# The output gate of a gated recurrence: multiplied by features in the output projection instead of by tokens in the recurrence

## The chip, the cores and the metric

The kernel runs on one core of one Trainium2 chip. The metric is the device time of one execution in microseconds; the time of a kernel is the median of its runs. A core has TensorE (PE in the profile, matrix products and transposes), VectorE (DVE), ScalarE (ACT), GpSimd (POOL) and SyncE (SP). SP does nothing here but issue loads, POOL issues the stores. Every engine executes its own instructions in the order in which they stand, and waits on semaphores for the others.

## What is computed

One layer of a language model on 2048 tokens of 1024 features. A combined input projection feeds two groups of heads, whose outputs are concatenated, multiplied by an output matrix and added to the residual with a layer norm behind it. The change lies in the first group, a gated linear recurrence with four heads of 128 features, of which this is the core:

```
h = jnp.einsum('btd,de->bte', h_res, w_in[layer])
hq, hf, hi, hg, aq, ak, av, ag = jnp.split(h, IN_SPLITS, axis=-1)
...
o_h = hgrn2_chunk(rs(q_h), rs(k_in), rs(hi.astype(f32)), rs(log_f))
o_h = o_h * lax.rsqrt(jnp.mean(o_h * o_h, axis=-1, keepdims=True) + RMS_EPS)
o_h = o_h * hg_norm_w[layer].astype(f32).reshape(HG_HEADS, HG_HEAD_DIM)
o_h = o_h.reshape(B, T, HG_WIDTH).astype(dt) * jax.nn.silu(hg)
...
mix = jnp.concatenate([o_h, o_a], axis=-1)
out = jnp.einsum('bte,ed->btd', mix, w_out[layer])
z = DN_ALPHA * h_res.astype(f32) + out.astype(f32)
```

`hi` are the values of the recurrence and `hg` its gate. The gate multiplies each head's normalised output, feature by feature.

## The kernel before

**Input projection.** The projection's columns are 26 feature tiles of 128 features, taken in 13 pairs. The tokens are two superblocks of 1024 (s = 0, 1), each two blocks of 512 tokens. One pair on one superblock is a 2x2 block product, computed with seven products of the Strassen-Winograd kind instead of eight: `px`, `py` and `pz` are its PSUM tiles, s1, s2, s5 and c10 the SBUF copies and sums that are formed from them, and `Pair.joined` (L364) adds a PSUM tile to such a copy. Every fp32 operand is split into a high and a low part of type fp32r, so a product is 12 matmuls of 128x512 (L342 to L344). A superblock takes 91 slots, one product each. The operand tiles of the weights (`w`) are made from loads of `in_wt_dram` in the first superblock and kept in DRAM (`kw`); the second superblock loads these 512 KB tiles.

**finish (L306).** A feature tile comes out with features on the partitions and 512 tokens along the row. `finish` stores it to DRAM as `proj[w][b]`, w being the feature tile and b the block of 512 tokens. Tiles 10 to 25 belong to the recurrence: of every eight (for a pair of heads j) two are forget gates (10, 11), two queries (12, 13), two values (14, 15) and two output gates (16, 17); 18 to 25 are the same for the second pair. They are stored as they are. Tiles 3, 4, 8 and 9, gates of the other group, go through SiLU by features first (`th`, L314 and L315: t · (1 + tanh(t/2)), the factor one half being left for later).

**Units.** Beside the products run 16 units of work, attached to slots by the table `units_at` (L790): 8 of `attend(j, b)`, which is the other group, and 8 of `recur(j, b)`. `recur` loads forget gates and queries (r10, r12, ...), forms decays by scans on DVE (`e`, L561 and L562), a reciprocal (L571) and the products `kq`. Its values and gates come by `fetch_vg` (four loads of 128 KB for two chunks of 128 tokens) and `vg`: for each chunk two heads' values and two heads' gates are transposed to have tokens on the partitions (eight transposes for two chunks), the values are copied out of PSUM by ACT, the gates get tanh on ACT and a product on DVE. `chunk` makes the outputs `ho` (L659), normalises them per token to `om`, multiplies by the gate (L675) and stores to `hg_spill`.

**Output stage.** There are 16 token tiles n of 128 tokens. `out_prepare(n)` is called one tile ahead: it loads the recurrence's output `mh` and the other group's output `ms` for these tokens, transposes the first in PE to features by tokens (`mp`, in a PSUM ring with one buffer, which the recurrence's `kp` shares), and splits both into high and low parts `m_0h`, `m_0l`, `m_1h`, `m_1l` (L724, L725). `out_tile(n)` does 48 matmuls of 128x512 into two PSUM tiles `po`, then residual and layer norm (`xr`). The output weights `wo` take the places of the input's operand tiles. Two of the recurrence's units still run while the first output tiles are computed.

**Order.** The program is written slot by slot, and a scheduler then sets the order of each engine's instructions by a list schedule with priorities; the joins and the copies of the products are marked high priority. A small change of the program can thus reorder work at a distance.

Of the kernel before, what the change touches and what calls it, by code (L numbers as in the profile page):

```python
# [13 lines left out]
AF = mybir.ActivationFunctionType  # L14
# [3 lines left out]
P = 128  # L18
# [26 lines left out]
def tile_hybrid_layer(  # L45
# [119 lines left out]
    def t_tile(name, dt=F32):  # L165
        return ring.tile([P, 512], dt, tag="t", name=name, bufs=9)
# [139 lines left out]
    def finish(pair, row, col, s, t):  # L306
        w, b = pair[col], 2 * s + row
        if w >= 10:
            nc.gpsimd.dma_start(proj[w][b], t)  # L309
            return  # L310
        j, kind = w // 5, w % 5
        if kind >= 3:
# [223 lines left out]
    def recur(j, b):  # L536
# [46 lines left out]
        def fetch_vg(pr):  # L583
            got["vg"] = []
            for i in range(2):
                t = t_tile(f"vg{j}_{b}_{pr}_{i}").rearrange("p (h t) -> p h t", t=2 * P)
                for h in range(2):
                    nc.sync.dma_start(t[:, h], proj[14 + 8 * j + 2 * i + h][b][:, pr * 2 * P : (pr + 1) * 2 * P])
                got["vg"].append(t)

        def vg(pr):
            raw = got["vg"]
            v4 = t_tile(f"hv{j}_{b}_{pr}").rearrange("p (s t) -> p s t", t=P)
            g4 = t_tile(f"hg{j}_{b}_{pr}").rearrange("p (s t) -> p s t", t=P)
            for i in range(2):
                c = 2 * pr + i
                ps = mm_ps(f"vg{j}_{b}_{c}").rearrange("p (s t) -> p s t", t=P)
                for s in range(4):
                    nc.tensor.transpose(ps[:, s, :], raw[s // 2][:, s % 2, i * P : (i + 1) * P], ident)
                nc.scalar.activation(v4[:, 2 * i : 2 * i + 2], ps[:, 0:2], AF.Copy)  # L600
                g = g4[:, 2 * i : 2 * i + 2]
                nc.scalar.activation(g, ps[:, 2:4], AF.Tanh, scale=0.5)
                nc.vector.scalar_tensor_tensor(g, g, 1.0, ps[:, 2:4], op0=ALU.add, op1=ALU.mult)
            got["v", pr] = v4, g4
# [31 lines left out]
        def chunk(c):  # L636
            pr, i = c // 2, c % 2
            at, kt = got["kt"]
            v4, g4 = got["v", pr]
# [35 lines left out]
            nc.vector.tensor_mul(om, om, g4)  # L675
# [7 lines left out]
            [lambda: factors(1), lambda: fetch_vg(0)],  # L683
            [],
            [lambda: vg(0), lambda: inner(0)],
            [lambda: chunk(0), lambda: fetch_vg(1)],
            [lambda: chunk(1)],
            [lambda: vg(1), lambda: inner(1)],
# [23 lines left out]
    def out_prepare(n):  # L712
# [7 lines left out]
        mp = mp.rearrange("p e t -> p (e t)")  # L720
        out_ = []
        for k, src in enumerate((mp, sw)):
# [210 lines left out]
```

## Time and profile before

| | before |
|---|---|
| time, median of 3 runs | 959.62 us (954.17 to 961.7) |
| the profiled execution's own time | 956.75 us |
| its span in the profile | 955.0 us |
| mean granted TensorE clock | 0.971 of full |

A profile is one execution. Its engines' rows say when an instruction ran and for how long; a matmul's row includes its latency, so neighbours overlap. "Granted clock" is the TensorE clock in parts of full speed.

### The profile page before, as it was taken

The numbers are of one execution on the slowest core, as the hardware profiler recorded it, in microseconds if no ns is written. First come the engines' busy times: TensorE is split into PE (matmuls) and PEld (weight loads), VectorE is DVE, ScalarE is ACT, GpSimd is POOL, SyncE is SP. The second block draws the span as 40 slices with busy tenths as digits, with TensorE's granted clock in tenths as the row PEclk, the third lists the DMA queues.
The fourth block names the chain that finished last, engine by engine and source line by source line (L and its number), as shares of the span: only waits on it lengthen the run. The fifth ranks groups of instructions, "written<-read, shape, count | busy, mean of one in ns | idle before, by whom it ended". The sixth has DMA issues, their size and how long they took to land.

```text
span 955.0 us, 14480 instructions
## 1 busy us (share of the span) xinstructions
PE 890.1 (93%) x4542; PEld 708.8 (74%) x4542; DVE 634.7 (66%) x1272; ACT 460.8 (48%) x1236; POOL 270.4 (28%) x444
## 2 busy tenths in 40 slices
PE   8478999999999999869999999989998999999995
PEld 6356777776778887658786768867787888888884
DVE  5977577575686589658565565445786889766554
ACT  5434455354553565428663535435576544544311
POOL 2224333333332222243422222222221232222211
PEclk9879999999999999979999999999999999999998
DMA  9289978675376675875958595475688534543222
GB/s 311 88 275 328 305 274 266 221 231 208 146 271 226 238 273 161 319 255 204 305 197 227 186 300 177 135 231 175 233 297 287 166 118 170 162 152 126 81 95 82
DMA packets 94493, 203.04 MB, mean 213 GB/s; under 512 B 13776, under 2 KB 31312, under 8 KB 94416
## 3 DMA queue, kind: packets, MB, share of 16 engines
q1 hardware_dynamic: 70448, 123.44, 41.9%
q0 software_dynamic: 23680, 78.15, 22.0%
q8 instruction: 36, 0.59, 0.3%
q10 hardware_dynamic: 288, 0.52, 0.1%
q14 instruction: 41, 0.34, 0.1%
HBM read 120.92 MB, written 78.64 MB: 209 GB/s over the span
## 4 chain that ended last, share of the span: by engine, by line
PE 70%; DMA 13%; DVE 9%; issue 3%; SPq 3%; ACT 2%; POOL 0%; DVEq 0%; POOLq 0%; ACTq 0%
PE px L342 7%; PE px L343 7%; PE px L344 7%; PE po L752 6%; PE po L753 6%; PE po L754 6%; PE pz L342 4%; PE pz L343 4%; PE pz L344 4%; DMA w<-in_wt_dram 3%; PE op L508 3%; DMA w<-kw 2%; PE sp L458 1%; PE sp L459 1%; PE hkv L647 1%
## 5 line engine op out<-in xcount | busy, mean ns | idle before, releaser
L309 POOL DMA_DIRECT2D proj<-s x48 | 26.6, 555 | 114.1 <-DVE s L364 86.3
L571 DVE RECIPROCAL f<-e 128x512 f32<-128x512 f32 x16 | 53.5, 3342 | 0.1
L359 ACT ACTIVATE s<-px 128x512 f32<-128x512 f32 x52 | 31.1, 598 | 45.3 <-PE px L344 37.7
L481 POOL TENSOR_TENSOR wt<-wt,st 128x512 f32<-128x512 f32 x32 | 34.0, 1062 | 62.1 <-DVE st L480 59.3
L472 ACT ACTIVATE wt<-sp,st 128x129 f32<-128x129 f32 x128 | 45.3, 369 | 4.1 <-DVE st L468 3.7
L766 ACT ACTIVATE xr<-xr,rs 128x512 f32<-128x512 f32 x32 | 24.3, 808 | 46.3 <-DVE rs L763 46.2
L185 DVE TENSOR_TENSOR w<-w,w 128x512 fp32r<-128x512 f32 x43 | 32.8, 769 | 16.3 <-ACT w L184 16.1
L755 DVE SCALAR_TENSOR_TENSOR xr<-xr,po 128x512 f32<-128x512 f32 x32 | 21.8, 682 | 29.8 <-PE po L754 27.7
L467 ACT ACTIVATE sp<-sink 128x2 f32<-128x2 f32 x64 | 11.1, 176 | 62.7 <-DVE st L464 59.1
L458 PE MATMUL sp<-kh,qa 128*128 128x256 f32 (+1 forms) x128 | 33.9, 295 | 7.2 <-DMA qa<-hl 5.6
L303 POOL DMA_DIRECT2D kw<-w x52 | 28.5, 547 | 39.7 <-DVE w L185 36.8
L342 PE MATMUL px<-x_s20h,w 128*128 128x512 f32 x26 | 12.2, 469 | 28.5 <-ACT w L184 23.8
L184 ACT ACTIVATE w<-w 128x512 fp32r<-128x512 f32 x43 | 26.9, 629 | 22.9 <-PE px L344 9.9
L463 DVE COPY_PREDICATED sp<-past,sp 128x256 f32<-128x256 int32 x60 | 24.6, 423 | 19.8 <-PE sp L459 19.6
L518 POOL DMA_DIRECT2D sw_spill<-mix x32 | 17.9, 561 | 63.6 <-DVE mix L517 51.8
L631 ACT ACTIVATE u<-s,e 128x128 f32<-128x128 f32 x60 | 21.4, 396 | 27.3 <-DVE s L656 22.9
L769 POOL DMA_DIRECT2D out_dram<-xr x30 | 17.6, 586 | 57.2 <-DVE xr L768 53.4
L493 ACT ACTIVATE pall<-pt 128x512 f32<-128x512 f32 x32 | 19.1, 596 | 30.1 <-PE pt L490 29.4
L459 PE MATMUL sp<-kl,qa 128*128 128x256 f32 (+1 forms) x128 | 33.4, 292 | 0.0
L517 DVE TENSOR_TENSOR mix<-op,gate 128x128 f32<-128x128 f32 x64 | 15.4, 282 | 26.9 <-PE op L508 26.1
L458 PEld LDWEIGHTS sp<-kh,qa 128*128 128x128 f32 x128 | 24.4, 193 | 11.8 <-DMA qa<-hl 7.9
L359 ACT ACTIVATE c<-px 128x512 f32<-128x512 f32 x26 | 15.6, 600 | 29.3 <-PE px L344 24.7
(506 smaller groups left out, 3169.1 us busy)
## 6 DMA issues: line engine op xcount, KB each, us to landing
kw<-w POOLq DMA_DIRECT2D x52, 512.0 KB, 4.8
w<-kw SPq DMA_DIRECT2D x52, 512.0 KB, 4.5
proj<-s POOLq DMA_DIRECT2D x60, 256.0 KB, 3.8
w<-in_wt_dram SPq DMA_DIRECT2D x47, 256.0 KB, 4.7
r<-proj SPq DMA_DIRECT2D x32, 256.0 KB, 4.2
vg<-proj SPq DMA_DIRECT2D x64, 128.0 KB, 4.1
xr<-in_xn_dram SPq DMA_DIRECT2D x32, 256.0 KB, 3.0
out_dram<-xr POOLq DMA_DIRECT2D x30, 256.0 KB, 2.5
```

Source lines behind the costliest of these rows:

```text
L342: nc.tensor.matmul(ps, lhsT=ah, rhs=bh, start=start, stop=False, skip_group_check=not first)
L343: nc.tensor.matmul(ps, lhsT=ah, rhs=bl, start=False, stop=False, skip_group_check=not first)
L344: nc.tensor.matmul(ps, lhsT=al, rhs=bh, start=False, stop=q == 3, skip_group_check=not first)
L359: nc.scalar.activation(t, ps, AF.Copy)
L458: nc.tensor.matmul(sp[:, h, lo:], lhsT=lhs, rhs=kh[:, kc], start=True, stop=False)
L459: nc.tensor.matmul(sp[:, h, lo:], lhsT=lhs, rhs=kl[:, kc], start=False, stop=True)
L472: nc.scalar.activation(wt_[:, s, :], sps[s // 2][:, s % 2, P - 1 :], AF.Exp, bias=st[:, 1, s : s + 1], scale=0.125, accum_out=st[:, 2, s : ...
L481: nc.gpsimd.tensor_mul(wt_[:, :, 1:], wt_[:, :, 1:], st[:, 0, :].unsqueeze(2).to_broadcast([P, 4, P]))
L571: nc.vector.reciprocal(re, e[:, :, 1:129])
L752: nc.tensor.matmul(ps, lhsT=h[:, q], rhs=wh, start=e == 0, stop=False)
L753: nc.tensor.matmul(ps, lhsT=h[:, q], rhs=wl, start=False, stop=False)
L754: nc.tensor.matmul(ps, lhsT=l[:, q], rhs=wh, start=False, stop=e == 7)
```

## The change

The gate tiles 16, 17, 24 and 25 go through SiLU in `finish`, by features, like the other group's gates. The recurrence then loads and transposes only values (`fetch_v`, `values`), eight fewer transposes in each of the eight units, and stores its outputs without the gate. In `out_prepare` the gate tile `gm` of the token tile is loaded (four loads of 64 KB, L712 of the changed kernel), and DVE multiplies the transposed outputs in PSUM with it; the high and low parts are split from the product in SBUF.

```diff
     def finish(pair, row, col, s, t):
         w, b = pair[col], 2 * s + row
-        if w >= 10:
+        if w >= 10 and (w - 10) % 8 < 6:
             nc.gpsimd.dma_start(proj[w][b], t)
             return
         j, kind = w // 5, w % 5
-        if kind >= 3:
+        if w >= 10 or kind >= 3:
             th = t_tile(f"th{w}_{b}")
...
-        def fetch_vg(pr):
-            got["vg"] = []
-            for i in range(2):
-                t = t_tile(f"vg{j}_{b}_{pr}_{i}").rearrange("p (h t) -> p h t", t=2 * P)
-                for h in range(2):
-                    nc.sync.dma_start(t[:, h], proj[14 + 8 * j + 2 * i + h][b][:, pr * 2 * P : (pr + 1) * 2 * P])
-                got["vg"].append(t)
-
-        def vg(pr):
-            raw = got["vg"]
+        def fetch_v(pr):
+            got["raw"] = t_tile(f"v{j}_{b}_{pr}").rearrange("p (h t) -> p h t", t=2 * P)
+            for h in range(2):
+                nc.sync.dma_start(got["raw"][:, h], proj[14 + 8 * j + h][b][:, pr * 2 * P : (pr + 1) * 2 * P])
+
+        def values(pr):
+            raw = got["raw"]
             v4 = t_tile(f"hv{j}_{b}_{pr}").rearrange("p (s t) -> p s t", t=P)
-            g4 = t_tile(f"hg{j}_{b}_{pr}").rearrange("p (s t) -> p s t", t=P)
-            for i in range(2):
-                c = 2 * pr + i
-                ps = mm_ps(f"vg{j}_{b}_{c}").rearrange("p (s t) -> p s t", t=P)
-                for s in range(4):
-                    nc.tensor.transpose(ps[:, s, :], raw[s // 2][:, s % 2, i * P : (i + 1) * P], ident)
-                nc.scalar.activation(v4[:, 2 * i : 2 * i + 2], ps[:, 0:2], AF.Copy)
-                g = g4[:, 2 * i : 2 * i + 2]
-                nc.scalar.activation(g, ps[:, 2:4], AF.Tanh, scale=0.5)
-                nc.vector.scalar_tensor_tensor(g, g, 1.0, ps[:, 2:4], op0=ALU.add, op1=ALU.mult)
-            got["v", pr] = v4, g4
+            ps = mm_ps(f"vp{j}_{b}_{pr}").rearrange("p (s t) -> p s t", t=P)
+            for s in range(4):
+                nc.tensor.transpose(ps[:, s, :], raw[:, s % 2, (s // 2) * P : (s // 2 + 1) * P], ident)
+            nc.scalar.activation(v4, ps, AF.Copy)
+            got["v", pr] = v4
...
-            nc.vector.tensor_mul(om, om, g4)
             nc.gpsimd.dma_start(
...
         for e in range(4):
             nc.tensor.transpose(mp[:, e, :], m[:, e * P : (e + 1) * P], ident)
-        mp = mp.rearrange("p e t -> p (e t)")
+        gated = t_tile(f"gm{n}").rearrange("p (e t) -> p e t", t=P)
+        for e in range(4):
+            nc.sync.dma_start(gated[:, e], proj[16 + 8 * (e // 2) + e % 2][n // 4][:, (n % 4) * P : (n % 4 + 1) * P])
+        nc.vector.tensor_mul(gated, mp, gated)
         out_ = []
-        for k, src in enumerate((mp, sw)):
+        for k, src in enumerate((gated.rearrange("p e t -> p (e t)"), sw)):
             h, l = m_split(src, f"m{n}_{k}")
```

The scheduler's order moves with it. In the rows below a name ends in a running number, and what an instruction waits for stands in brackets. The first place is the start of the second token superblock, SP's loads; `w1_0_7` is an operand tile of superblock 1, pair 0, product 7, and `r10_1` the forget gates of block 1. Before:

```order
L287 DMA w1_0_7_3858<-kw0_7_226 128x1024 [waits DMASW5_49,DMASW7_49,DMASW2_49,PE_49]
L259 DMA w1_8_1a_4357<-in_wt_dram 128x512 [waits DMAHW5_49,DVE_49]
L287 DMA w1_0_4_3920<-kw0_4_223 128x1024 [waits DMASW3_49,DMAHW6_49,DMASW2_49,PE_49]
L542 DMA r10_1_3881<-proj10_1_160 128x512 [waits DMAHW7_49,Pool_49]
L542 DMA r12_1_3883<-proj12_1_168 128x512 [waits DMAHW0_49]
L287 DMA w1_1_6_3964<-kw1_6_229 128x1024 [waits DMAHW1_49,PE_49]
```

After, on the same engine:

```order
L287 DMA w1_0_7_3852<-kw0_7_226 128x1024 [waits DMASW7_49,DMAHW0_49,DMASW4_49,PE_49]
L287 DMA w1_0_4_3914<-kw0_4_223 128x1024 [waits DMASW2_49,DMAHW1_49,DMASW0_49,PE_49]
L287 DMA w1_1_6_3958<-kw1_6_229 128x1024 [waits DMAHW4_49,DMAHW2_49,PE_49]
L259 DMA w1_8_1a_4333<-in_wt_dram 128x512 [waits DMAHW3_49,DVE_49]
L542 DMA r10_1_3875<-proj10_1_160 128x512
L542 DMA r12_1_3877<-proj12_1_168 128x512 [waits DMAHW5_49,Pool_49]
```

The loads r10_1 and r12_1 have moved behind w1_1_6, and w1_8_1a behind w1_1_6 as well. In the same place on DVE, before; `e0_1` are the scans, `s5_1_0` the joins of superblock 1, pair 0:

```order
L561 SCALAR_TENSOR_TENSOR e0_1_3879<-f0_1_3886 128x64
L364 TENSOR_TENSOR s5_1_0_3979<-px1_0_3681,s5_1_0_3979 128x512
L562 SCALAR_TENSOR_TENSOR e0_1_3879<-f0_1_3886 128x64
...
L185 TENSOR_TENSOR l6_2_3915<-s1_1_6_3800,h6_2_3914 128x512
L571 RECIPROCAL f0_1_3886<-e0_1_3879 128x512
L577 SCALAR_TENSOR_TENSOR r12_1_3883<-tq0_1_3939,r12_1_3883 128x512
L364 TENSOR_TENSOR s2_1_0_3934<-pz1_0_3966,s2_1_0_3934 128x512
```

And after:

```order
L562 SCALAR_TENSOR_TENSOR e0_1_3873<-f0_1_3880 128x64
L185 TENSOR_TENSOR l6_2_3909<-s1_1_6_3794,h6_2_3908 128x512
L571 RECIPROCAL f0_1_3880<-e0_1_3873 128x512
L577 SCALAR_TENSOR_TENSOR r12_1_3877<-tq0_1_3933,r12_1_3877 128x512
L364 TENSOR_TENSOR s5_1_0_3973<-px1_0_3675,s5_1_0_3973 128x512
L185 TENSOR_TENSOR w1_1_3_4048<-w1_2_1_3956,w1_1_3_4048 128x512
L364 TENSOR_TENSOR s2_1_0_3928<-pz1_0_3960,s2_1_0_3928 128x512
```

The join s5_1_0 has moved from between the first scans to behind the reciprocal and r12's product. The second place is the head of the output stage, SP's loads before:

```order
L716 DMA mh0_7446<-hg_spill0_0_95 128x256 [waits DMAHW2_49,DVE_49]
...
L716 DMA mh1_7465<-hg_spill0_1_96 128x256
L588 DMA vg0_3_1_0_7546<-proj14_3_178 128x256 [waits DMAHW5_49,Pool_49]
L716 DMA ms1_7466<-sw_spill1_0_65 128x256 [waits DMAHW6_49,DVE_49]
L716 DMA ms1_7466<-sw_spill1_1_66 128x256 [waits DMAHW7_49]
L588 DMA vg0_3_1_0_7546<-proj15_3_182 128x256 [waits DMAHW0_49]
```

After, on SP:

```order
L706 DMA mh0_7330<-hg_spill0_0_95 128x256 [waits DMAHW4_49,DMAHW1_49,DVE_49]
...
L706 DMA mh1_7355<-hg_spill0_1_96 128x256
L735 DMA xr0_0_7384<-in_xn_dram 128x512 [waits DMASW7_49,DMASW4_49,DMAHW7_49,DMASW2_49,DMASW0_49]
L706 DMA ms1_7356<-sw_spill1_0_65 128x256 [waits DMAHW1_49,DMAHW2_49,DMAHW0_49,PE_49]
L706 DMA ms1_7356<-sw_spill1_1_66 128x256
L712 DMA gm0_7341<-proj16_0_183 128x128
L712 DMA gm0_7341<-proj17_0_187 128x128 [waits DMAHW3_49]
L712 DMA gm0_7341<-proj24_0_215 128x128 [waits DMAHW4_49]
L712 DMA gm0_7341<-proj25_0_219 128x128 [waits DMAHW5_49]
```

The gate loads gm0 stand behind the loads ms1, whose wait is now for PE (its transposes mp0) where it was for DVE. PE at the same place, before:

```order
L719 MATMUL mp0_7452<-ident_294,mh0_7446 128x128
L659 MATMUL ho0_3_0_7528<-hv0_3_0_7395,at0_348 128x128 [waits DVE_49,Activation_49]
...
L659 MATMUL ho0_3_0_7528<-hv0_3_0_7395,at0_348 128x128
L752 MATMUL po0_0_7493<-wo_a110h_7125,m0_0h_7457 128x512 [waits Activation_49]
L753 MATMUL po0_0_7493<-wo_a110l_7126,m0_0h_7457 128x512
```

And after:

```order
L709 MATMUL mp0_7336<-ident_294,mh0_7330 128x128
L650 MATMUL ho0_3_0_7424<-hv0_3_0_7287,at0_348 128x128 [waits DVE_49,Activation_49]
...
L650 MATMUL ho0_3_0_7424<-hv0_3_0_7287,at0_348 128x128
L709 MATMUL mp1_7361<-ident_294,mh1_7355 128x128 [waits DMAHW5_49,DVE_49]
L709 MATMUL mp1_7361<-ident_294,mh1_7355 128x128
...
L745 MATMUL po0_0_7389<-wo_a110h_7023,m0_0h_7347 128x512 [waits Activation_49]
```

The four transposes mp1 of the second token tile now stand ahead of the first output product po0_0, with a wait for DVE.

## Rows read from the trace of the kernel before

**Rows 1.** The page, busy time of each engine, share of the span, instructions.

```profile
PE 890.1 (93%) x4542; PEld 708.8 (74%) x4542; DVE 634.7 (66%) x1272; ACT 460.8 (48%) x1236; POOL 270.4 (28%) x444
```

**Rows 2.** Windows: PE, PEld, DVE, ACT, POOL busy; granted clock; DMA share; GB/s.

```profile
350.00:380.00 30.00, 30.00 (x134) 24.84 (x133) 29.90 (x50) 17.65 (x32) 5.24 (x8) 1.00 0.54 184
380.00:425.00 45.00, 33.24 (x146) 25.57 (x145) 27.72 (x53) 16.35 (x32) 16.09 (x24) 0.89 0.79 277
...
700.00:725.00 25.00, 25.00 (x155) 21.09 (x154) 20.82 (x39) 19.45 (x45) 5.18 (x11) 1.00 0.94 315
725.00:735.00 10.00, 7.19 (x38) 6.09 (x36) 6.72 (x13) 7.45 (x23) 2.33 (x3) 0.83 0.96 294
735.00:945.00 210.00, 210.00 (x1082) 172.50 (x1080) 143.33 (x276) 83.32 (x211) 51.06 (x88) 1.00 0.41 134
```

**Rows 3.** Waits of PE: us in total, times, longest us.

```profile
PE sp L458 <- DMA qa<-hl: 5.6, 2, 3.9
PE px L342 <- DMA w<-kw: 4.7, 2, 4.4
...
PE ho L659 <- ACT om L674: 2.7, 1, 2.7
...
PE pz L342 <- DMA w<-kw: 2.0, 1, 2.0
```

**Rows 4.** The chain of waits from 376 to 426 us: start, us, what.

```profile
379.12 7.80 DMA r<-proj
...
391.21 3.34 DVE f L571
...
416.65 0.44 PE vg L599 x4
417.09 0.23 PE px L342
...
418.48 5.37 DMA w<-kw
...
425.12 0.43 PE px L344
```

**Rows 5.** Groups by line and shape: count, busy us, mean ns, idle before.

```profile
L599 PE MATMUL vg<-ident,vg 128*128 128x128 f32 x128 | 17.8, 276 | 0.0
L603 DVE SCALAR_TENSOR_TENSOR hg<-hg,vg 128x256 f32<-128x256 f32 x32 | 12.8, 410 | 1.9 <-ACT hg L602 1.5
...
L600 ACT ACTIVATE hv<-vg 128x256 f32<-128x256 f32 x32 | 12.3, 387 | 5.9 <-PE vg L599 5.9
...
L675 DVE TENSOR_TENSOR om<-om,hg 128x512 f32<-128x512 f32 x16 | 11.0, 689 | 12.2 <-ACT om L674 12.1
...
L724 ACT ACTIVATE m_0h<-mp 128x512 fp32r<-128x512 f32 x16 | 9.6, 599 | 26.9 <-PE mp L719 26.8
...
L315 DVE SCALAR_TENSOR_TENSOR s<-th,s 128x512 f32<-128x512 f32 x12 | 8.6, 726 | 1.1 <-ACT th L314 1.0
...
L314 ACT ACTIVATE th<-s 128x512 f32<-128x512 f32 x12 | 7.4, 625 | 1.9 <-DVE s L364 1.9
```

**Rows 6.** Line L588, loads of values and gates: ns min/median/max of an issue; landing.

```profile
L588 SPq DMA_DIRECT2D vg<-proj x64: 319/423/1622, 279.7 to 841.9; - x64
...
DMA to landing us min/median/max: 2.2/4.1/8.6
```

**Rows 7.** DMA issues: count, KB each, median us to landing.

```profile
mh<-hg_spill SPq DMA_DIRECT2D x32, 128.0 KB, 2.6
```

**Rows 8.** PE's timeline: start, us, instruction [idle before <-releaser].

```profile
389.47 0.50 PE L342 MATMUL px<-x_a220h,w 128*128 128x512 f32 x1 [2.04 <-DVE s L364]
...
725.08 0.60 PE L719 MATMUL mp<-ident,mh 128*128 128x128 f32 x4
...
730.41 0.79 PE L752 MATMUL po<-wo_a110h,m_0h 128*128 128x512 f32 x1
```

More of the change, by code (lines that the diff above doesn't have):

```diff
@@ L638, in chunk @@
             at, kt = got["kt"]
-            v4, g4 = got["v", pr]
+            v4 = got["v", pr]
             if c == 0:
@@ L682, in recur @@
             [lambda: factors(0), lambda: decays(1)],
-            [lambda: factors(1), lambda: fetch_vg(0)],
+            [lambda: factors(1), lambda: fetch_v(0)],
             [],
-            [lambda: vg(0), lambda: inner(0)],
-            [lambda: chunk(0), lambda: fetch_vg(1)],
+            [lambda: values(0), lambda: inner(0)],
+            [lambda: chunk(0), lambda: fetch_v(1)],
             [lambda: chunk(1)],
-            [lambda: vg(1), lambda: inner(1)],
+            [lambda: values(1), lambda: inner(1)],
             [lambda: chunk(2)],
```

## The prediction

> **What bounds the kernel now.** I begin with the page's line of busy time: TensorE (PE) is busy 890.1 us of a span of 955.0, 93% [rows 1]. What the other engines do pays only where it makes PE wait, and an instruction taken from PE pays in full wherever PE is the one that ends last. Then the table of windows, which tells the stretches apart [rows 2]. From 735 to 945 us, the output stage, PE is busy all of 210.00 us at a granted clock of 1.00, with VectorE (DVE) at 143.33, ScalarE (ACT) at 83.32 and the DMA rings at a share of 0.41: nothing but PE's own columns bounds it. Three stretches are different. Just before the second token superblock (350 to 380) PE is full, but so is DVE, 29.90 of 30. Over the change of superblock (380 to 425) PE has only 33.24 of 45 and a clock of 0.89; at the head of the output stage (725 to 735) it has 7.19 of 10 and 0.83. A granted clock of 1.00 is 2.4 GHz, half of it 1.2 GHz; 0.83 over 10 us is some 3.4 us at the lower level, and in both places the fall follows idle time of PE. Last the waits of PE [rows 3] and the chain through the change of superblock [rows 4]: the chain there runs over the load of the recurrence's rows (7.80 us), the reciprocal (3.34) and a weight load (5.37), not over PE's columns.
>
> **What is taken away.** The order of the changed kernel has 4024 matmuls and transposes on PE for 4088: 64 transposes fewer. The trace has two prices for one. A single transpose lasts 276 ns in the mean [rows 5], but transposes overlap: in the chain four of them take 0.44 us together [rows 4], 0.11 each. The path is charged the second. So 64 × 0.11 = 7.0 us. Of this the eight transposes of the unit for head pair 0 and token block 0 (0.9 us) fall before the load that the chain waits for at the change of superblock; PE would only come to that wait sooner, so I give them back. On ACT the change drops 64 reads of 128x256 from PSUM, 32 copies at 387 ns and 32 tanh of the same shape, 64 × 0.39 = 25.0 us, and adds 16 copies of 128x512 (0.60 as in the copies of mp) and 16 tanh by features (0.625): 19.6 [rows 5]. On DVE it drops 32 products at 410 ns and 16 gate products at 689 ns, 24.1 us, and adds 16 products by features (726 ns, 11.6) and 16 products with PSUM in the output stage (689, 11.0). These net gains of 5.4 and 1.5 us count nothing: neither engine is the bound in the long stretches [rows 2]. If PE were not the cover in 735 to 945, the 16 products would cost at most 11.0 us; with 143.33 of 210 busy before, DVE has 67 us for them.
>
> **What is added to the queue of loads.** SP issues 32 loads fewer (gates and values together 64 before, now 32 for values alone) and 64 gate loads of 64 KB. One issue takes 0.42 us in the median [rows 6], so 64 − 32 = 32 more are 13 us of SP's time, nearly all in 735 to 945, where the rings have a share of 0.41 [rows 2]; each token tile there lasts 210/16 = 13 us, and its four gate loads take 1.7 us of issue and, by loads of 128 KB, 2.6 to 8.6 us to land [rows 6, 7]. Both fit a tile that is prepared one ahead, so I charge nothing after the first tile. Were the cover gone, a tile would wait for the part of 1.7 + 8.6 that exceeds 13, still nothing.
>
> **What is moved: the change of superblock.** The scheduler puts things in another order here, in two ways that matter. SP now issues the weight load w1_1_6 (512 KB, behind a wait for PE) and w1_8_1a (behind a wait for DVE) before r10_1, the load that heads the chain. And DVE gets the join s5_1_0 behind the reciprocal and r12's product instead of before them: 3.34 + 0.7 = 4.0 us later, after a load that may itself be later. Before, PE waited 2.04 us for this join [rows 8]. Now PE has the product px1_0.a22 behind pz1_1.s1 and the kp transposes, so at least one product of twelve matmuls of 512 columns (0.23 us each [rows 4], 2.8) fills the gap. Besides, DVE gets four products of gates by features (0.726 each) and loses one gate product (0.689) in the stretch where it was full [rows 2]: +2.2 us. No row shows the new arrangement, so I bound it: at best the moved product covers it all and the old 2.04 us shrinks as well (0, or up to 2 gained); at worst 4.0 − 2.8 + 2.2 = 3.4, with some of the columns after it at 1.2 GHz, 4. I take +1.5, nearer to the best end, because the chain is at a load at that time [rows 4] and the four products need not lie on it.
>
> **What is moved: the head of the output stage.** Before, the transposes mp0 began at 725.08 [rows 8], at 0.44 for four through by 725.5; ACT's copy m_0h has work of the recurrence ahead of it in its queue, and the first output product po0_0 began at 730.41, 4.9 us after mp0. Now that copy needs the gated product, which needs the loads gm0, and SP has these behind the two loads ms1, which wait for PE's mp0. So, from mp0's end: two issues of ms1 (0.8), four of gm0 (4 × 0.42 = 1.7), landing, the product (0.69), the copy (0.60). For the landing the nearest rows are loads of 128 KB, 2.6 us (mh [rows 7]) and 4.1 (the values and gates [rows 6]); a gm load has half the bytes, so I take 3.1, near the first. That is 6.9 us, 2.0 more than 4.9. PE also has the transposes mp1 in front of po0_0 now, which wait for the same gated product (they reuse its PSUM buffer), so nothing else fills the gap. I add 1.0 for the clock, which is at 0.83 here already, and 0.5 for ACT and DVE, which do other work in the same place: +3.5. At best the old wait of PE for ho (2.67 [rows 3]) hides it: 0. At worst the landing is the longest of the values' loads, 8.6 [rows 6], in a ring with a share of 0.96: 0.8 + 1.7 + 8.6 + 1.3 = 12.4, 7.5 more than before, with the clock 8.
>
> **The sum.** −7.0 + 0.9 + 1.5 + 3.5 = −1.1 us. The profiled execution took 956.75 us, so it would be 955.65; it lies 2.9 us below the median of the three timed runs, 959.62 (954.17 to 961.7). The time is compared with the median, so I forecast 959.62 − 1.1 = **958.5 us**. From the ends of the unknown terms the forecast's own range is −7 + 0.9 − 2 = −8.1 to −7 + 0.9 + 4 + 8 = +5.9, 951.5 to 965.5. A change below 1% (9.6 us) is about what the measurement of this kernel can't tell from none.
>
> **Rivals.** First, *the saving comes through whole and waits shrink with it*. The recurrence's fetches are halved during the superblocks, and PE waits there for loads: 5.6 + 4.7 + 2.0 = 12.3 us [rows 3]. If a third of it went, 4 us, and neither moved place cost anything, the change is −7 − 4 = −11: 948.6. For it: the rings' share of 0.79 and 0.94 where these waits lie [rows 2]. Against it: the gates' bytes come back later, and the order there is worse for r10_1.
>
> Second, *a transpose costs PE its duration*. Then 64 × 0.276 = 17.6 are gained and the result is about 942. Against it speaks the row of four in 0.44 us: at 0.276 each they would take 1.1 [rows 4, 5]. The Trainium skill, "TensorE: Matmul & The Clock Gate", in its passage on PE-mode transposes, gives about 275 ns for one in a kernel's context, mostly latency of access; that agrees with the trace's 276, but by the same trace it is a latency that neighbours share, not time taken from the engine.
>
> Third, on the other side, *DVE and the queue hold PE at both places*. The join s5_1_0 and r10_1 are both late, so that the change of superblock costs the reciprocal with what stands around it, 6 us, and 3 us more at 1.2 GHz (0.43 for 0.23 a matmul [rows 4], some 15 of them); and the gates land late at the head of the output stage, 8. The sum is −7 + 0.9 + 9 + 8 = +10.9: 970.5. It decides from the point where r10_1 is issued later than the end of DVE's last join before it, so that nothing covers the reciprocal. For it: DVE is full at 29.90 of 30 [rows 2], and all engines run in order, so that a late load holds what stands behind it. Against it: PE has a product to put in between, and before the load was as long as 7.80 us without costing more than the waits in the list.
>
> That the change does not do what it says is excluded for the count (64 fewer on PE), not for the effect: that is the forecast itself.
>
> **How the numbers follow.** The forecast has 0.59, the first rival 0.19, the second 0.03, the third 0.19. The range leaves out 2 in 10: from below the first rival, 947, to the third's, 971. Of the first rival most lies beyond 1% (950.0), with the second and a little of the forecast's low end 0.20; of the third nearly all lies at or above 969.2, 0.18; the rest, 0.62, is within 1%.
>
> **What would show it.** In the changed profile the transposes' line should have half its count at the same pitch, 0.44 per four, and 735 to 945 should stay full on PE from its first tile to its last. At the change of superblock PE's wait for a join (2.04) should be replaced by one of similar size for r10_1's chain; at the head of the output stage a wait of PE for DVE's gated product of some 2 us should be seen, with po0_0 about 6.9 us after mp0. I would be wrong if PE waited for gate loads in later tiles, if waits in the superblocks moved by more than 4 us in either direction, or if the rearranged order elsewhere cost or gave more than the two places that I priced.

## The result, and the profile of the changed kernel

The changed kernel takes 965.11 us in the median of 11 runs (958.07 to 970.9), the kernel before 959.58 (954.17 to 961.7, 11 runs): a ratio of 1.007, interval 1.0046 to 1.0095. The medians differ by 5.5 us, and by the interval the changed kernel is slower by 4.4 to 9.1 us, where 1.1 us less was forecast. Within 1% is where the time lies and what had the largest chance, and it lies inside the range, but on the other side and clear of noise.

The profiled execution of the changed kernel took 967.24 us with a span of 965.5, that of before 956.75 and 955.0: these two differ by 10.5 us, more than the medians do. The page's line of busy time, which answers to [rows 1], shows that the change did what it says:

```profile
PE 888.5 (92%) x4478; PEld 703.8 (73%) x4478; DVE 634.0 (66%) x1256; ACT 459.5 (48%) x1204; POOL 274.5 (28%) x444
```

PE has 64 instructions fewer; ACT (460.8 to 459.5) and DVE (634.7 to 634.0) lost a little busy time. Only POOL is busy longer, by 4.1 us, with the same 444 instructions. So the busy time does not show where the loss is. The table of windows of the changed kernel, columns as in [rows 2], tells where it is:

```profile
380.00:425.00 45.00, 33.44 (x146) 25.34 (x144) 27.78 (x53) 15.62 (x28) 16.13 (x23) 0.92 0.76 266
425.00:700.00 275.00, 259.31 (x1392) 203.37 (x1393) 150.37 (x338) 137.12 (x420) 76.41 (x118) 0.97 0.67 206
```

and the second of these stretches in the kernel before, which the prediction did not look at:

```profile
425.00:700.00 275.00, 265.90 (x1458) 210.36 (x1457) 160.00 (x360) 144.31 (x457) 78.20 (x120) 0.99 0.70 219
```

The change of superblock (380 to 425) has kept its 33 us of PE. In 425 to 700, PE went from 9.1 us without work to 15.7, and its granted clock from 0.99 to 0.97. The waits of PE in the changed kernel, which answer to [rows 3] (us in total, times, longest):

```profile
PE sp L458 <- DMA qa<-hl: 9.0, 3, 5.1
PE px L342 <- DMA w<-kw: 8.9, 3, 5.1
PE ho L650 <- ACT om L665: 3.4, 1, 3.4
...
PE sp L458 <- DMA vt<-vals: 2.9, 1, 2.9
PE pz L342 <- DMA w<-kw: 2.8, 1, 2.8
```

`sp` are the attention's scores, `qa`, `kh`, `kl` and `vt` its queries, keys (high and low part) and values. The waits for `qa`, `vt` and `w` come to 23.6 us where they were 12.3 [rows 3] and 0.5 for `vt`.

The lag of one execution behind the other can be read by following single instructions. Here are PE's stops in the timeline of the kernel before, start, us, instruction, idle before:

```profile
132.31 0.50 PE L342 MATMUL px<-x_s30h,w 128*128 128x512 f32 x1 [0.75 <-ACT s L359]
...
423.90 0.80 PE L342 MATMUL px<-x_s20h,w 128*128 128x512 f32 x1 [4.43 <-DMA w<-kw]
473.47 0.48 PE L458 MATMUL sp<-kh,qa 128*128 128x256 f32 x2 [0.71 <-PE px L344]
...
511.73 0.36 PE L458 MATMUL sp<-kh,qa 128*128 128x256 f32 x1 [1.72 <-DMA qa<-hl]
562.02 0.50 PE L342 MATMUL pz<-x_s10h,w 128*128 128x512 f32 x1 [2.03 <-DMA w<-kw]
626.83 0.58 PE L458 MATMUL sp<-kh,qa 128*128 128x256 f32 x1 [3.85 <-DMA qa<-hl]
728.34 0.49 PE L659 MATMUL ho<-hv,at 128*128 128x128 f32 x2 [2.67 <-ACT om L674]
```

and the same instructions in the changed kernel, with the head of the output stage (the transposes mp0, mp1 and the first output product):

```profile
134.75 0.50 PE L342 MATMUL px<-x_s30h,w 128*128 128x512 f32 x1 [0.75 <-ACT s L359]
...
426.28 0.79 PE L342 MATMUL px<-x_s20h,w 128*128 128x512 f32 x1 [5.14 <-DMA w<-kw]
479.08 0.55 PE L458 MATMUL sp<-kh,qa 128*128 128x256 f32 x1 [5.07 <-DMA qa<-hl]
519.14 0.36 PE L458 MATMUL sp<-kh,qa 128*128 128x256 f32 x1 [3.67 <-DMA qa<-hl]
572.13 0.50 PE L342 MATMUL pz<-x_s10h,w 128*128 128x512 f32 x1 [2.79 <-DMA w<-kw]
...
733.89 0.78 PE L709 MATMUL mp<-ident,mh 128*128 128x128 f32 x4 [0.29 <-ACT th L314]
738.09 0.49 PE L650 MATMUL ho<-hv,at 128*128 128x128 f32 x2 [3.41 <-ACT om L665]
741.66 1.11 PE L709 MATMUL mp<-ident,mh 128*128 128x128 f32 x4 [1.37 <-DVE gm L713]
742.43 0.78 PE L745 MATMUL po<-wo_a110h,m_0h 128*128 128x512 f32 x1
```

The differences of the starts are 2.4 us at 132, where both programs are still alike (so this is scatter), 2.4 at 424, 5.6 at the scores of attention block 2, 7.4 at those of block 3, 10.1 at 562, 9.8 at `ho` and 12.0 at the first output product (730.41 before [rows 8]); the end is 10.5 apart. In this pair nothing is lost up to 424. Some 8 us go between 424 and 562, 2 more up to the first output product, and a little comes back behind it.

Why the scores of block 2 wait is seen in SP's timeline. First the kernel before, some of the loads ahead of these scores:

```profile
452.83 0.48 SPq L413 DMA_DIRECT2D qa<-hl  x1
...
468.16 0.42 SPq L413 DMA_DIRECT2D qa<-hl  x1
468.63 1.43 SPq L415 DMA_DIRECT2D qa<-hl  x2
...
471.79 0.48 SPq L409 DMA_DIRECT2D kl<-kl  x1
...
473.43 0.67 SPq L259 DMA_DIRECT2D w_0a<-in_wt_dram  x1
```

then the changed kernel:

```profile
454.94 0.33 SPq L259 DMA_DIRECT2D w_0a<-in_wt_dram  x1
...
467.94 0.81 SPq L413 DMA_DIRECT2D qa<-hl  x1
468.90 0.83 SPq L415 DMA_DIRECT2D qa<-hl  x2
469.77 0.43 SPq L413 DMA_DIRECT2D qa<-hl  x1
472.74 0.48 SPq L409 DMA_DIRECT2D kl<-kl  x1
473.26 1.06 SPq L415 DMA_DIRECT2D qa<-hl  x2
```

Half of the queries' loads have moved from the start of the unit's 20 loads to their end, a weight load (`w_0a`) has moved ahead of all of them, and the last two query loads stand behind the copy `kl<-kl`, which first waits for loads to land (SP issues nothing from 470.2 to 472.7). The last query load is issued at about 473.8 where it was 469.6, and the scores start 5.6 us later. None of these loads belongs to the change; the scheduler moved them.

### The profile page after: what moved, and what is told of

The parts are those of the page before. It is cut to its first block, busy times and chain, and to the rows that moved or that the text cites. A ratio compares the mean times of both kernels' runs of the same rounds, so it can differ in the third digit from the quotient of the medians.

```text
span 965.5 us, 14327 instructions
## 1 busy us (share of the span) xinstructions
PE 888.5 (92%) x4478; PEld 703.8 (73%) x4478; DVE 634.0 (66%) x1256; ACT 459.5 (48%) x1204; POOL 274.5 (28%) x444
## 4 chain that ended last, share of the span: by engine, by line
PE 59%; DMA 16%; DVE 11%; issue 5%; ACT 4%; SPq 3%; POOL 1%; DVEq 0%; POOLq 0%; ACTq 0%
PE px L342 7%; PE px L343 7%; PE px L344 7%; PE pz L342 4%; PE pz L344 4%; PE pz L343 4%; PE po L747 3%; PE po L745 3%; PE po L746 3%; PE op L508 3%; DMA qa<-hl 2%; PE sp L458 2%; PE sp L459 2%; DMA w<-kw 1%; DMA x_r<-in_xt_dram 1%
## 5 line engine op out<-in xcount | busy, mean ns | idle before, releaser
L309 POOL DMA_DIRECT2D proj<-s x36 | 20.0, 555 | 79.5 <-DVE s L364 62.1
L458 PEld LDWEIGHTS sp<-kh,qa 128*128 128x128 f32 x128 | 24.8, 195 | 16.7 <-issue 10.1
L185 DVE TENSOR_TENSOR w<-w_1a,w 128x512 fp32r<-128x512 f32 x35 | 27.2, 777 | 9.2 <-ACT w L184 9.0
L762 POOL DMA_DIRECT2D out_dram<-xr x30 | 17.6, 585 | 53.1 <-DVE xr L761 46.4
L342 PEld LDWEIGHTS px<-x_s20h,w 128*128 128x128 f32 x26 | 5.3, 202 | 37.1 <-ACT w L184 26.3
```

What stands on the lines that cost most here:

```text
L185: nc.vector.tensor_sub(l, src, h.bitcast(F32))
L342: nc.tensor.matmul(ps, lhsT=ah, rhs=bh, start=start, stop=False, skip_group_check=not first)
L458: nc.tensor.matmul(sp[:, h, lo:], lhsT=lhs, rhs=kh[:, kc], start=True, stop=False)
```

## The experiments

The theory after this reading was that the changed order of loads makes the loss between 424 and 562, and the late gate load the one at the head of the output stage. The rival was that the work itself (SiLU by features, a product more in the output stage, gate loads in busier rings) makes it whatever the order. Ratios below are to the kernel before, timed on the same chip.

**A second profile of each kernel**, unchanged.

> The changed kernel once more, for a second profile. Theory (the loss sits in waits that the changed order makes): the waits of PE for the attention's queries return where they were, near 5.1 us for block 2 and 3.7 us for block 3, and so do the two at the head of the output stage (3.4 and 1.4 us), each within 1 us. Rival (one disturbed execution): some of them are gone, and with them the excess over the kernel before.

> The kernel before once more, for a second profile, to see how far single waits differ between two executions of one program. Theory: the waits of PE for the attention's queries and weights between 425 and 700 us stay within 1.5 us of the first profile in sum (about 9 us). Rival: they vary by as much as the two kernels differ (5 us and more).

The changed kernel again, 962.09 us in its single run:

```profile
477.30 0.55 PE L458 MATMUL sp<-kh,qa 128*128 128x256 f32 x1 [4.92 <-DMA qa<-hl]
516.84 0.36 PE L458 MATMUL sp<-kh,qa 128*128 128x256 f32 x1 [3.32 <-DMA qa<-hl]
```

The kernel before again, 956.92 us:

```profile
471.84 0.48 PE L458 MATMUL sp<-kh,qa 128*128 128x256 f32 x2 [0.34 <-PE px L344]
475.02 0.46 PE L435 MATMUL vp<-ident,vt 64*128 64x64 f32 x4 [0.81 <-DMA vt<-vals]
510.00 0.36 PE L458 MATMUL sp<-kh,qa 128*128 128x256 f32 x1 [1.26 <-issue]
```

The waits return: 4.9 and 3.3 us in the one program, 0.3, 0.8 and 1.3 in the other (`issue` stands where the profile shows nothing that PE waited for). They belong to the programs, not to one execution. At the head of the output stage the changed kernel again had 2.86 and 1.01 us. Single places scatter by 1 to 2 us. With two profiles of each kernel the loss can be read by stretches, each between the starts of the same two instructions (us; "head" is from the first of the transposes mp0 to the first output product, and the end is that of the span):

| stretch | before | before again | changed | changed again | difference of the means |
|---|---|---|---|---|---|
| 132 to 424 | 291.6 | 288.9 | 291.5 | 292.7 | +1.8 |
| 424 to 562 | 138.1 | 137.6 | 145.9 | 144.2 | +7.1 |
| 562 to mp0 | 163.1 | 163.5 | 161.8 | 160.0 | −2.4 |
| head | 5.3 | 5.0 | 8.5 | 8.6 | +3.4 |
| first output product to the end | 224.6 | 226.6 | 223.1 | 222.6 | −2.8 |

The stretch from 424 to 562 is 32 products, 384 matmuls, with what stands between them. By the same count, from the start of the first to the start of the one behind the last, it can be read in every other run below.

**The queries ahead of the key copy.** In the changed kernel, for blocks 2 and 3 of the first head group:

```diff
-                nc.sync.dma_start(t[64:128, w0:].bitcast(F32), t[0:64, w0:].bitcast(F32))
+                if (j, part) != (0, 1) or b < 2:
+                    nc.sync.dma_start(t[64:128, w0:].bitcast(F32), t[0:64, w0:].bitcast(F32))
...
+            if j == 0 and b >= 2:
+                behind(nc.sync.dma_start(kl[64:128, w0:].bitcast(F32), kl[0:64, w0:].bitcast(F32)), last)
```

`behind` adds an edge of issue order and no wait; `last` is the last load of the queries. The scheduler takes the edge into account and then sets the order of all engines anew. So in this experiment, and in all that follow except the last two, PE, DVE and ACT also run in another order from the edited place on, with the same instructions.

> The changed kernel, with only the queue order altered: for the attention's blocks 2 and 3 of the first head group all loads of the queries are issued ahead of the copy of the low key part, which waits for loads to land. Theory (queue order): PE's wait for the queries of block 2 falls from 5.1 to about 2.5 us, that of block 3 from 3.7 to about 2, and the time falls by about 4 us, to a ratio of 1.003 to the kernel before. Rival (the loads land late because the rings are busier, whatever the order): the waits stay above 4 and 3 us and the ratio stays at 1.007.

Measured 969.01 us, ratio 1.0114 (1.0075 to 1.0153). The two stops:

```profile
474.58 0.77 PE L469 MATMUL sp<-kh,qa 128*128 128x256 f32 x2 [3.99 <-DMA qa<-hl]
514.61 0.76 PE L469 MATMUL sp<-kh,qa 128*128 128x256 f32 x2 [5.10 <-issue]
```

The first wait fell by 1.1 us only, the second grew by 1.4, and the total did not gain; the 32 products take 151.1 us. The theory in this narrow form falls: the copy ahead of two query loads is not the whole cause. The scores need the copied keys as well, so what is put first only changes which of the loads is last; that this is the reason is argued, not shown.

**The late order in the kernel before**: its last two query loads of block 2 are put behind the copy.

```diff
+                    if (j, b, part) == (0, 2, 1):
+                        behind(last, copy)
```

> The kernel before, with only the queue order altered: the last two loads of the queries of block 2 of the first head group are put behind the copy of the low key part, as the changed kernel has them. Theory (queue order): a wait of PE for these queries of 3 to 5 us appears where there was 0.7, and the ratio is 1.003 to 1.005. Rival (the order is harmless): no wait above 1 us there, ratio 1.000.

Measured 969.4 us, ratio 1.0102 (1.0076 to 1.0128), and 147.5 us for the 32 products. At block 2:

```profile
474.76 0.56 PE L445 MATMUL vp<-ident,vt 64*128 64x64 f32 x4 [3.33 <-DMA vt<-vals]
...
479.56 0.28 PE L468 MATMUL sp<-kh,qa 128*128 128x256 f32 x1
```

The expected wait for the queries is not there. The scheduler has put the transposes of `vt` ahead of the scores, where they stood behind them (471.84 and 475.02 in the second profile of before), and PE waits 3.33 us for `vt`, where it was 0.5 to 0.8. Block 3 now waits 3.27 us for its queries (1.72 and 1.26 before) and the weights of the pair behind it 4.66 us (2.03 and 1.75). So an edit of issue order that changes no work costs 1%, about as much as the whole change did. That the order is not harmless is shown, at two to three times the size expected. That it is the order of the two loads is not: the other engines' order moved with it.

**The gates of token tile 0 ahead of tile 1's loads**, in the changed kernel:

```diff
+                if n == 1:
+                    behind(load, gm_last[0])
```

> The changed kernel, with only the queue order altered at the head of the output stage: the gates of token tile 0 are loaded ahead of the recurrence's and attention's outputs of tile 1. Theory (the chain over the late gate load costs some 3 us there): the first output product starts 5 to 6 us after the first transposes of the output stage instead of 8.5, and the ratio falls from 1.007 to about 1.004. Rival (ACT's work in front of the split sets the start, not the load): it still starts about 8 us after them, ratio 1.007.

Measured 971.93 us, ratio 1.0107 (1.0072 to 1.0141). The first output product waited longer, not less:

```profile
747.42 0.80 PE L757 MATMUL po<-wo_a110h,m_0h 128*128 128x512 f32 x1 [4.50 <-ACT m_0h L729]
```

The edit, which also writes every tile's gate loads ahead of its other loads, moved more than it meant to: both loads of `xr0` went ahead of the gates. This profile had also lost 2.9 us more than the changed kernel's by 429 us, and 5.8 us more by 578, where the two programs are alike. It says nothing on the gate load itself; the early gates, further below, do. But by 705 us this kernel, that with early gates and the two profiles of the changed kernel run their instructions in one order, so their 32 products give four executions of it: 145.9, 144.2, 148.7 and 147.1 us, against 138.1 and 137.6 in the order of before.

**The old order of loads.** Instead of single edits, the changed kernel's loads were held to the order of the kernel before up to the output stage; the order of PE, DVE and ACT was left to the scheduler. A table gives each instruction's place in the program as written; consecutive ones get an edge of issue order:

```diff
+    order = json.loads(zlib.decompress(base64.b64decode(ORDER)))
+    ins = list(nc.cur_bb.bb.instructions)
+    for seq in order.values():
+        for a, b in zip(seq, seq[1:]):
+            tc.add_manual_dep(
+                ins[b],
+                ins[a].name,
+                mybir.DependencyInfo(mybir.DependencyClass.NoSync, mybir.DependencyReason.DATA),
+                reason="order",
+            )
```

> The changed kernel's work, with the loads on SP's queue held to the order of the kernel before up to the output stage (70% of the queue; loads that only the changed kernel has stand where they followed their neighbour); the other engines' order is left to the scheduler. Theory (the order of the loads makes the loss in the second superblock): PE's waits for the attention's queries of blocks 2 and 3 fall to 1 to 2 us from 5.1 and 3.7, and the ratio falls from 1.007 to about 1.000, with 3 us still lost at the head of the output stage. Rival (the changed work itself, or the other engines' order, makes it): the ratio stays at 1.006 or more.

> As the one with the old order of loads, and TensorE too is held to the order of the kernel before over the first 40% and from 60 to 70% of its instructions. Theory (the order of the loads is what matters, PE follows): within 0.3% of the kernel with the old loads alone, about 1.000. Rival (PE's own order is a cause of its own): at least 0.4% below that one.

> The work of the kernel before, with all loads on SP's queue held to the changed kernel's order (the gates' loads, which the changed kernel does not have there, follow their neighbours). Theory (the order of the loads): the waits of PE for the attention's queries grow to 4 to 5 us and 3 to 4 us, and the ratio is 1.008 to 1.015. Rival (the changed work itself): 1.000 to 1.003.

With the old order of loads, 960.71 us, ratio 1.0019 (0.9993 to 1.0046):

```profile
478.47 0.47 PE L458 MATMUL sp<-kh,qa 128*128 128x256 f32 x2 [1.34 <-issue]
516.61 0.36 PE L458 MATMUL sp<-kh,qa 128*128 128x256 f32 x1 [3.71 <-DMA qa<-hl]
...
736.48 1.11 PE L709 MATMUL mp<-ident,mh 128*128 128x128 f32 x4 [5.20 <-DVE gm L713]
```

0.51% or 4.9 us come back. The wait at block 2 is 1.34 us instead of 5.07; the one at block 3 stayed. The 32 products take 137.8 us, as in the kernel before, but in this profile they begin 294.8 us after the mark at 132, and the head takes 9.6. With PE held too it is 964.72 us, ratio 1.0053 (1.0031 to 1.0074): not a gain but a loss of 0.34%, with intervals that overlap, and 143.7 us for the 32 products. That fits neither expectation. SP's queue has the same order in these two kernels, so the order of PE, DVE and ACT can be worth about as much as the loads'.

The reverse, the work of the kernel before with the changed kernel's order of loads, takes 975.74 us, ratio 1.0181 (1.0162 to 1.0201), more than the theory asked, with 152.4 us for the 32 products:

```profile
484.90 0.55 PE L458 MATMUL sp<-kh,qa 128*128 128x256 f32 x1 [7.12 <-DMA qa<-hl]
526.86 0.37 PE L458 MATMUL sp<-kh,qa 128*128 128x256 f32 x1 [3.26 <-issue]
```

The kernel before does 64 transposes more and, with this order, is slower than the changed kernel. So the order is a cause without the changed work, in both directions: with the old order of loads the changed work takes 137.8 us for the 32 products, with the new one the work of before takes 152.4. It is the order of the loads together with the one that the scheduler sets for the other engines; which part each has, no run shows.

**Early gates.** The gate tiles take two buffers that the projection's sums leave free, and the first two are loaded 8 slots ahead of the output stage:

```diff
-        gated = t_tile(f"gm{n}").rearrange("p (e t) -> p e t", t=P)
-        for e in range(4):
-            nc.sync.dma_start(gated[:, e], proj[16 + 8 * (e // 2) + e % 2][n // 4][:, (n % 4) * P : (n % 4 + 1) * P])
+        gated = gates.pop(n)
...
+        if g == 2 * NS - 8:
+            load_gate(0)
+            load_gate(1)
```

> The changed kernel, with the gate tiles in two buffers of their own kind (the ones that the projection's temporary sums leave free) and the first two loaded some 8 slots before the output stage; each later one is loaded as soon as its buffer is free. Theory (the chain over the late gate load costs about 3 us at the head of the output stage, and nothing else there): no wait of PE for a gated product above 1 us there, the first output product 5 to 6 us after the first transposes, ratio 1.003 to 1.004. Rival (other work of the stage's head sets the start): still 8 us after them, ratio 1.006 or more.

> The same with early gates, and the loads on SP's queue held to the order of the kernel before over the first 70% of the queue. Theory (the loss has two parts, the order of the loads in the second superblock and the late gate load, and the 64 transposes are worth about 7 us): both parts gone, ratio 0.994 to 0.998. Rival (the transposes are worth less than 7 us on the path, or their time goes into the next wait): 0.999 to 1.003.

Early gates alone: 962.96 us, ratio 1.005 (1.0022 to 1.0078), 0.2% below the changed kernel, with intervals that overlap. In its profile mp0 starts at 731.61 and the first output product at 738.65, 7.0 us later where it was 8.5, and mp1 waits for the gated product at another place:

```profile
735.14 0.66 PE L718 MATMUL mp<-ident,mh 128*128 128x128 f32 x4 [2.57 <-DVE gm L720]
```

That lies between the theory's 5 to 6 and the rival's 8, and a wait of more than 1 us for the gated product is left. The gate load was one part of the wait; the other is that mp0 and mp1 share a PSUM buffer, so mp1 needs DVE to be through with mp0. DVE is busy without a break from 730.05 to 735.68, with other work in front, and begins this product only here:

```profile
734.40 0.69 DVE L720 TENSOR_TENSOR gm<-mp,gm 128x512 f32<-128x512 f32 x1
```

With the old order of loads as well: 956.08 us, ratio 0.999 (0.9963 to 1.0017), 0.29% below the one with the late gates, with intervals that overlap. Both edits together regain 0.8% over the changed kernel, yet the result is no faster than before, where the theory wanted 0.994 to 0.998. In its profile (960.55 us, 4.5 above its median) the 32 products take 140.3 us, the head 6.1 with PE waiting 1.34 and 2.58 us for loads of `mh`, and block 3 still waits:

```profile
474.26 0.77 PE L458 MATMUL sp<-kh,qa 128*128 128x256 f32 x2 [2.14 <-DVE w L185]
514.29 0.36 PE L458 MATMUL sp<-kh,qa 128*128 128x256 f32 x1 [4.04 <-DMA qa<-hl]
```

**More room for the attention's loads.** To see whether PE takes the saved time there as waiting, an idle step of two slots was put between the loads and the first scores of the four late attention units, in the kernel before and in the improved one, both with the old order of loads:

```diff
             [fetch],
+            *([[]] if b >= 2 else []),
             [values, lambda: score(0)],
```

> The kernel before, with one idle step of two slots between the loads and the first scores of the four attention units of the second token half, and SP's loads held to the old order over 70% of the queue. It is the control of the next kernel. Theory (PE waits there because the 20 loads of a unit take longer than the step): the waits of PE for the attention's inputs fall from 7 us in sum to under 3, ratio 0.994 to 0.998. Rival (they move into the next wait): 0.999 to 1.002.

> The changed work with early gates and the old order of loads, with the same idle step. Theory (the time of the removed transposes went into the waits for the attention's loads, whose chain does not get shorter): with the step it shows, and the kernel is 0.5 to 0.8% below the control, 0.987 to 0.992. Rival (it is lost at the change of superblock and at the head of the output stage, whatever the attention does): within 0.3% of the control.

955.83 us and 0.9995 (0.9964 to 1.0027) for the control, 956.89 us and 0.9984 (0.9957 to 1.0012) for the changed work. The waits of the scores at blocks 2 and 3 are gone in both, and each has a new one at 560 us, for the weights, whose load stands behind the attention's in SP's queue. The control:

```profile
561.38 0.77 PE L342 MATMUL px<-x_s20h,w 128*128 128x512 f32 x1 [5.18 <-DMA w<-kw]
```

and the changed work:

```profile
559.54 0.77 PE L342 MATMUL px<-x_s20h,w 128*128 128x512 f32 x1 [5.56 <-DMA w<-kw]
```

Both rivals held: room at one wait opened another, and the two kernels stay within 0.3%. Here too the step changed the order of the engines along with the room.

**What the 64 transposes are worth.** The last two kernels are the only ones in which one thing alone differs. They are the kernel before with every engine held to its order instruction by instruction, with the gates' transposes left out and with them done twice:

```diff
-                for s in range(4):
+                for s in range(2):
                     nc.tensor.transpose(ps[:, s, :], raw[s // 2][:, s % 2, i * P : (i + 1) * P], ident)
```

> The kernel before with the 64 transposes of the gates left out, and every engine held to its order instruction by instruction; the gate's tanh and product read the transposed values in their place, so the output gate is computed from the wrong tensor and only the time counts. Theory (PE waits for loads in the second superblock, and takes the saved time there as waiting): 2 to 4.5 us less, ratio 0.995 to 0.998. Rival (each transpose saves its 0.11 us of pitch on the path): 7 us less, ratio 0.9925 or below.

> The kernel before with the 64 transposes of the gates done twice, all else in the old order. Theory (the waits for loads take part of it up): 2 to 5 us more, ratio 1.002 to 1.005. Rival (full pitch on the path): 7 us more, 1.0075.

Without them: 955.22 us, ratio 0.997 (0.9941 to 0.9998), 2.9 us less, and at most 5.7 by the interval. Twice: 964.57 us, 1.0052 (1.0027 to 1.0076), 5.0 us more, and 2.6 to 7.3 by the interval. The kernel without them, at the places where it waits:

```profile
469.82 0.48 PE L458 MATMUL sp<-kh,qa 128*128 128x256 f32 x2 [1.65 <-DMA qa<-hl]
473.02 0.46 PE L435 MATMUL vp<-ident,vt 64*128 64x64 f32 x4 [1.27 <-DMA vt<-vals]
508.60 0.36 PE L458 MATMUL sp<-kh,qa 128*128 128x256 f32 x1 [1.84 <-issue]
```

Against the second profile of the kernel before, the waits at these three grew from 0.34, 0.81 and 1.26 us to 1.65, 1.27 and 1.84, by 2.4 us (1.9 against the first profile). The 32 products take 139.3 us without these transposes, no less than the 138.1 and 137.6 with them. So in this stretch the saving goes into waiting. By the medians the transposes are worth 3 to 5 us on this path; the theory holds. Leaving them out excludes the full 7 us, doubling them does not.

## Why the prediction was wrong

**The order in the second superblock was not priced.** The failed step is the limit the prediction set itself: it costed the moved order at two places and let everything between them, and SP's queue after the fewer loads of the recurrence, count nothing. [rows 2] has no row for 425 to 700, and 7.6 of the 12.3 us of waits in [rows 3] lie there: 1.72 at 512, 2.03 at 562 and 3.85 at 627. In place of that zero the profiles show +7.1 us between 424 and 562, which alone turns −1.1 into a loss. The runs agree on the side: −4.9 us for the changed kernel with the old order of loads (1.007 to 1.0019), +17 us for the kernel before with the new one, each with the other engines set anew. It was named at the end as what would make it wrong ("if the rearranged order elsewhere cost or gave more than the two places that I priced"), without a price.

**64 × 0.11 = 7.0, of which 0.9 is given back, was probably too much.** The count was right, and the pitch holds for PE's own time: PE is busy 8.3 us less without the transposes and 6.0 more with them doubled. But only 2.9 us reach the end of the program at a fixed order (5.7 at most by the interval, 5.0 for the doubled ones). The 0.9 us that were given back belong to one unit; by the 139.3 us for the 32 products without transposes, the units between 424 and 562 give theirs back too, where PE only arrives sooner at the waits for loads. The saving shows behind 562, where the changed kernel is faster by 2.4 and 2.8 us outside the head.

**The head of the output stage** was forecast at +3.5 with 6.9 us from the end of mp0 to po0_0. The profile has 733.89 to 742.43, 8.5 from start to start where it was 5.3: +3.2, and +3.4 with the second pair. The mechanism stood as described: gm0 is issued behind ms1, lands after 3.2 us (3.1 taken), is multiplied and copied, and mp1 waits for the product (1.37 us). What the prediction put at only 0.5 us is the other work of DVE and ACT there: with the gates early it is DVE's other work that holds the product, and the two kernels with early gates are only 0.2 to 0.3% below those with late ones.

**The change of superblock**, +1.5 forecast, is not at fault: +1.8 between 132 and 424 us, within the scatter of two profiles.

**ACT, DVE and the later gate loads** cost little: DVE −0.7 and ACT −1.3 us of busy time where −1.5 and −5.4 were worked out. Behind the first two token tiles PE stops for 0.5 us at most in the first profile of the changed kernel, and once for 1.02 us, for a gated product, in the second.

**The rivals.** The second (276 ns each, 17.6 us) is out by the price measured. The first (a third of the waits for loads goes) had the sign wrong: these waits nearly doubled. Its argument also misread [rows 2]: the DMA share of 0.94 belongs to 700 to 725, where none of these waits lies; in 425 to 700, where three of them lie, it is 0.70. The third was right in the side and in saying that a late load holds what stands behind it on an in-order engine, but it put 9 us at r10_1 and the join, where 1.8 were lost, and 8 at the head, where it was 3.4.

**What stays open.** With the transposes at −3 to −5, the old order of loads at 4.9 and the gates at the head at +2 to +3, the sum is +2 to +5, against 5.5 by the medians and 6.7 by the ratio. With both edits the kernel is at −1 (−3.5 to +1.6) where −3 to −5 should be left. Part of the difference lies where these edits did not do all they were meant to: 140.3 us for the 32 products and a head of 6.1; the rest was not found. How the loss between 424 and 562 is shared between the order of the loads and that of PE, DVE and ACT is open: no run has the changed kernel's loads with every other engine in the old order, nor the changed work with the old order on all engines. No kernel here that keeps the whole computation beats the one before by more than its interval.

## What to carry to other kernels

A change that takes work from the busiest engine saves that work's time only as far as no wait for something unchanged comes behind it: look for the next place where that engine waits for a load, and give the saving back there. Where a scheduler sets the order, compare every engine's order and the whole queue of loads, not only the places that the edit touches; here the loss lay behind units with 20 small loads in one queue. An edge that holds one engine's order lets the scheduler move the others, so compare their orders in the two traces before you call it the effect of that edge. To price an edit by itself, hold every engine to the old order and take out, or double, the edited work alone.

## What was not expected of the hardware

An edge that moves two loads in SP's queue cost 1.0%, and the full new order of loads 1.8%, with the same instructions and bytes; in both the scheduler also moved the other engines' instructions. The time went into PE's stops (3 to 7 us each) for the loads of the attention and of the weights. In the kernel before, the 20 loads of an attention unit take 17.5 us from the first issue (494.23) to the scores (511.73), 12.9 of them until the last is issued, though the rings' share in that stretch is only 0.77.
